# Turning attention weights two units at a time in a merged stage of a hybrid attention layer

## The chip, the cores and the metric

The kernel runs on one core of one Trainium2 chip. The metric is the device time of one execution in microseconds (us); less is better. The core has TensorE (PE: matmuls and transposes), VectorE (DVE), ScalarE (ACT), GpSimd (POOL) and SyncE (SP, which issues most DMAs).

## The reference

One layer for 1024 tokens of width 1024. From the normed input come the operands of two kinds of heads; their outputs are normed, gated, multiplied by `w_out`, normed again and added to the input. The change touches the differential attention of the first kind, 8 heads of width 128:

```python
s = jnp.einsum('bqhmd,bkhmd->bhmqk', qb, k).astype(jnp.float32)   # two maps m per head
p = jax.nn.softmax(jnp.where(mask, s, -jnp.inf), axis=-1)          # causal
w = p[:, :, 0] - lam * p[:, :, 1]
out = jnp.einsum('bhqk,bkhv->bqhv', w.astype(v.dtype), v)
...
oa = rms_norm(oa, subln_g) * (1.0 - lam_init)
oa = oa.reshape(B, S, DA_WIDTH) * jax.nn.silu(ga)
```

The second kind (4 heads of gated linear attention) and the input projection are finished before the stage that the change is in.

## The kernel before

**The stages.** Up to about 645 us the kernel norms the input, multiplies it by `w_in` and runs the linear-attention heads. Then comes a merged stage with all the softmax attention and a part of the product with `w_out`, and at the end the rest of that product, the last norm and the output. To keep float32 accuracy at the speed of the rounded type, each operand of a matmul is split in a high and a low part (`hi`, `lo`), and a product is three matmuls: hi·hi, hi·lo, lo·hi.

**The merged stage.** Three Python generators write its instructions, and `merge` (line 1048) interleaves them: each has a clock of its own, every `yield` of a number moves that clock on by this cost, and the stream with the earliest clock writes next. A `yield` of a function halts its stream until the function holds. Matmuls and transposes are kept in the order in which they are written; the order on ACT, DVE and POOL is fixed when the program is built, and each engine runs its instructions in that order.

- `all_scores` (line 1165): for each head, query blocks of 128 rows from 7 down to 0. `scores` multiplies q by k and ks (the two parts of k) into a bank `sc`, of which three go round; DVE masks and reduces it (L1137) into a row tile `p0` or `p1`; ACT takes the exponential (L1147); POOL (L1153) and DVE (L1152, L1156) combine both maps into the weights, which stay in `p0`. A row over 512 wide has two score pairs. Query blocks 0 to 5 have one `p0` tile each, so the next head's scores of block 5 and of block 3 wait in the stream until the weights of the head before are turned (L1168).
- `all_values` (line 1253): the weights lie with queries on the partitions and must lie with keys there. A **unit** is one key block (or the last two) of one half of a head's queries: ten per head, seven for the upper half (query blocks 4 to 7), three for the lower. `turn` (line 1185) transposes a unit in 3 or 4 transposes into one of two banks `wtr` (`tr_bank` takes them in turns), ACT casts it to `wt_hi` (L1195) and DVE subtracts to `wt_lo` (L1196), three buffers each. `weigh` (line 1199) multiplies it by v into the bank `po`, in three matmuls per key block.
- When a half is complete, ACT copies `po` to `o` (L1290), and `attn_norm` (line 1213) norms it in steps, one per call of `norm_step`: the first squares it on ACT (L1225, L1226), adds on DVE (L1227) and splits the sum into `sq_hl` on ACT (L1228) and DVE (L1229); the fifth sums over the partitions with the matmul `ms`, which takes the next of the two `wtr` banks, and does the rest. In what follows the *upper* and *lower norm* are those of a head's upper and lower half.
- `out_early` (line 1357): parts of the product with `w_out` into the banks `ypart`, a triple of 512-wide matmuls at a time. It fills PE between the other two.

Before the change `all_values` turns one unit at each unit, two ahead of the one that it weighs. Each turn and each weighing is followed by one norm step.

Of the kernel before, what the change touches and what calls it, by code (L numbers as in the profile page):

```python
# [20 lines left out]
DA_HEADS = 8  # L21
# [10 lines left out]
def hymba_kernel(  # L32
# [23 lines left out]
    def fp(t):  # L56
        return t.bitcast(F32)
# [46 lines left out]
    def bank(i, shape, name):  # L104
        return psum.tile(shape, F32, tag=f"b{i}", name=name)
# [13 lines left out]
    def tr(dst, src):  # L119
        tc.keep_in_program_order(pe.transpose(dst, src, ident))  # L120
# [114 lines left out]
    i = order.index((1, 4))  # L235
# [847 lines left out]
    def load_v(h):  # L1083
        v = [smp.tile([P, NT, P], F32R, tag="v", name=f"v{t}", bufs=4) for t in range(2)]
        for t in range(2):

            with tc.issue_after(qk_load[0]) if h else nullcontext():
                ins = sp.dma_start(fp(v[t]), v_d[h // 4][h % 4, t])
            if h == 0:
                tc.keep_in_program_order(ins)  # L1090
        return v
# [9 lines left out]
    def tr_bank(name, shape):  # L1101
        n_tr[0] += 1
        return bank(TR[n_tr[0] % 2], shape, name)
# [77 lines left out]
    def blocks_of(kt, half):  # L1181

        return range(max(kt - 4 * half, 0), 4)

    def turn(h, half, kts):

        pt = tr_bank("wtr", [P, 512])
        n = 0
        for kt in kts:
            for i in blocks_of(kt, half):  # L1190
                tr(pt[:, n : n + P], w[h, 4 * half + i][:, kt * P : (kt + 1) * P])
                n += P
        hi = smp.tile([P, 512], F32R, tag="wt_hi", name="wt_hi", bufs=3)
        lo = smp.tile([P, 512], F32R, tag="wt_lo", name="wt_lo", bufs=3)
        act.copy(hi[:, :n], pt[:, :n])  # L1195
        dve.tensor_tensor(lo[:, :n], pt[:, :n], fp(hi[:, :n]), ALU.subtract)  # L1196
        return hi, lo

    def weigh(po, half, kts, v, wt):

        hi, lo = wt
        n = 0
        for kt in kts:
            ns = len(blocks_of(kt, half)) * P
            for i, (a, b) in enumerate(((v[0], hi), (v[1], hi), (v[0], lo))):
                mm(
                    po[:, 512 - ns :], a[:, kt, :], b[:, n : n + ns],
                    start=(kt == 0 and i == 0), stop=(kt >= 4 * half and i == 2),
                    skip_group_check=True,
                )  # L1210
            n += ns

    def attn_norm(h, half, o):
        if h < DA_HEADS - 1:
            gate = smp.tile([P, 512], F32, tag="gate", name="gate", bufs=2)
        else:
            gate = kp.tile([P, 512], F32, tag=("q1", "k1")[half], name="gate")
        with tc.issue_after(qk_load[0]):
            sp.dma_start(gate, g_d[h][:, cols(half)])
        sq = smp.tile([P, 512], F32, tag="r", name="sq", bufs=1)  # L1220


        hl = smp.tile([P, 512], F32R, tag="sq_hl", name="sq_hl", bufs=1)
        fold = smp.tile([P, 512], F32, tag="fold", name="fold", bufs=1)
        act.activation(fold[:64], o[64:], AF.Square)  # L1225
        act.activation(sq[:64], o[:64], AF.Square)  # L1226
        dve.tensor_tensor(sq[:64], sq[:64], fold[:64], ALU.add)  # L1227
        act.copy(hl[:64], sq[:64])  # L1228
        dve.tensor_tensor(hl[64:], sq[:64], fp(hl[:64]), ALU.subtract)  # L1229
        if h == DA_HEADS - 1:  # L1230

            dve.scalar_tensor_tensor(gate, o, sub_g, gate, ALU.mult, ALU.mult)
        for _ in range(4):
            yield 0.0
        n_tr[0] += 1
        ms = bank(TR[n_tr[0] % 2], [P, 512], "ms")
        mm(ms, ones, hl, start=True, stop=True)
        if h == DA_HEADS - 1 and not half:
            opened[TR[n_tr[0] % 2]] = None
        r = smp.tile([P, 512], F32, tag="r", name="r", bufs=1)  # L1240
        act.activation(r, ms, AF.Ln, bias=eps_t, scale=1.0 / P)
        act.activation(r, r, AF.Exp, scale=-0.5)
        if h < DA_HEADS - 1:
            dve.scalar_tensor_tensor(r, o, sub_g, r, ALU.mult, ALU.mult)
            pool.tensor_tensor(gate, r, gate, ALU.mult)
            sp.dma_start(mixd[h * P : (h + 1) * P, cols(half)], gate)
            stored.append(h)
        else:
            dve.tensor_tensor(gate, gate, r, ALU.mult)
            last_mix[half] = gate  # L1250
        yield 0.0

    def all_values():


        AHEAD = 2
        units = [
            (h, half, kts) for h in range(DA_HEADS) for half in (1, 0)
            for kts in [(k,) for k in range(4 * half + 2)] + [(4 * half + 2, 4 * half + 3)]
        ]  # L1260
        vs, os, turned, norms_todo = {0: v_first}, {}, {}, []
        ahead = iter(units)

        def norm_step():
            while norms_todo:
                c = next(norms_todo[0], None)
                if c is not None:
                    return
                norms_todo.pop(0)

        for i, (h, half, kts) in enumerate(units):
            last = kts[-1] == 4 * half + 3

            ahead_by = AHEAD if h < DA_HEADS - 1 else AHEAD
            while len(turned) < min(i + 1 + ahead_by, len(units)):
                u = next(ahead)
                if u[2] == (0,):
                    yield lambda: (u[0], 4 * u[1]) in w
                turned[u] = turn(*u)
                if u[2][-1] == 4 * u[1] + 3:  # L1280
                    used.add(u[:2])
                yield 0.4
                norm_step()
            if kts == (0,):
                o = smp.tile([P, 512], F32, tag="o", name="o", bufs=3)
                po = bank(PO, [P, 512], "po")
            weigh(po, half, kts, vs[h], turned[h, half, kts])
            norm_step()
            if last:
                act.copy(o, po)  # L1290
                if half and h + 1 < DA_HEADS:
                    vs[h + 1] = load_v(h + 1)
                norms_todo.append(attn_norm(h, half, o))
            yield 0.6

            if i == 1:
                yield SOON * DA_HEADS * 10.0 / T
        carry = norms_todo[-1]
        while len(norms_todo) > 1:
            norm_step()  # L1300
        next(carry)
        yield 0.0
        yield lambda: (ENDS[2], 0) in ps_d
        early_ends()
        yield from carry
# [144 lines left out]
    def early_ends():  # L1450

        for e in range(4, 7):
            last_times(ENDS[2], 0, parts_d[ENDS[2]], e)
        for st in ENDS[:2]:
            last_part(st, parts_d[st])
            for dh in range(2):
                last_times(st, dh, parts_d[st], 7)
        seed(ENDS[2], 1, PO, sums_of(2)[:, 1])
        for st in ENDS[2:4]:
            last_part(st, parts_d[st])  # L1460
# [19 lines left out]
    def last_times(st, dh, part, e):  # L1480
# [14 lines left out]
    merge(  # L1495
        [0.0, T, DA_HEADS * s_cost, all_scores()],
        [LAG - SOON, T + LAG, DA_HEADS * 10.0 * (1 + SOON / T), all_values()],
        [-6.0, T + LAG + 20, 16.0 + 14 * 5.52 + 16 * 2.76 + 11.8, out_early()],
    )
# [124 lines left out]
```

## Time and profile before

| | us |
|---|---|
| three runs, median (lowest to highest) | 974.5 (973.81 to 975.0) |
| the profiled execution | 972.62 |
| its span, first to last instruction | 970.9 |
| PE busy in the span | 951.4 |
| transposes `wtr`, first and last start | 646.4 and 916.4 |

A row of the timeline has the start in us from the span's beginning, the duration in us, the engine, the line of the kernel, the operation, the tile written and the tiles read, the shape and how many were merged into the row; in brackets stands how long the engine had been idle and what released it. A row of a group has busy time and the mean in ns of one; a row of one tile's view has the shortest, the median and the longest duration in ns. Matmuls overlap, so their cost is read from start to start. A matmul's line is 117 and a transpose's 120, whoever called them: they are told apart by their tiles.

### The profile page before, as it was taken

To read this page: it belongs to the slowest core of one execution; us is meant where nothing else is said; L and a number is where in the kernel's file an instruction comes from. 1 tells how busy PE (TensorE), PEld (TensorE's weight loads), DVE (VectorE), ACT (ScalarE), POOL (GpSimd) and SP (SyncE) were. 2 spreads that over 40 slices of the span, in tenths; PEclk is the share of its full clock that TensorE was granted. 3 is DMA by queue.
4 is the path that set the end of the run, shared out by engine and by line. 5 is a ranking of instruction groups with operands and counts; after the bars stand their busy time and mean duration, and the time that the engine had idled before them with its cause. 6 is when DMAs were issued, how large, how long until landed. Compare 5 with 4: busy or idle time off the path is not lost.

```text
span 970.9 us, 15022 instructions
## 1 busy us (share of the span) xinstructions
PE 951.4 (98%) x4946; PEld 810.2 (83%) x4946; DVE 734.9 (76%) x1462; ACT 602.9 (62%) x1164; POOL 205.0 (21%) x263
## 2 busy tenths in 40 slices
PE   6999999999999999999999999999999999999997
PEld 5998988888888888888888888878888888888785
DVE  6986599897687686686766576587888888898554
ACT  8642464764667565576765344366786777887773
POOL 5300001212141221231100002121322222443322
PEclk9999999999999999999999999999999999999999
DMA  9442456478668987996854589988656669995777
GB/s 357 142 124 89 130 171 225 174 247 275 216 202 262 286 277 252 293 293 208 259 184 144 169 249 287 385 273 267 220 172 227 231 201 352 335 293 102 153 210 146
DMA packets 152301, 220.39 MB, mean 227 GB/s; under 512 B 16752, under 2 KB 87408, under 8 KB 152128
## 3 DMA queue, kind: packets, MB, share of 16 engines
q1 hardware_dynamic: 138128, 178.80, 57.2%
q0 software_dynamic: 14096, 40.64, 14.7%
q8 instruction: 39, 0.64, 0.3%
q14 instruction: 38, 0.31, 0.1%
HBM read 133.93 MB, written 88.60 MB: 229 GB/s over the span
## 4 chain that ended last, share of the span: by engine, by line
PE 94%; DVE 3%; ACT 1%; DMA 1%; issue 1%; POOL 0%; SPq 0%; DVEq 0%; ACTq 0%
PE x L117 23%; PE y L117 15%; PE z L117 15%; PE ypart L117 13%; PE sc L117 7%; PE po L117 5%; PE yps L117 4%; PE wtr L120 3%; PE gpo L117 3%; PE kv L117 1%; PE gkl_ps L117 1%; PE pa L117 1%; DMA k_d<-qk_st 1%; PE xT L120 1%; ACT junk L574 0%
## 5 line engine op out<-in xcount | busy, mean ns | idle before, releaser
L352 ACT CAST w<-w_raw 128x512 fp32r<-128x512 f32 (+1 forms) x150 | 98.1, 655 | 91.5 <-PE y L117 47.1
L353 DVE TENSOR_TENSOR w<-w_raw,w 128x512 fp32r<-128x512 f32 (+1 forms) x150 | 109.6, 734 | 40.5 <-ACT w L352 40.1
L1147 ACT ACTIVATE p<-p,stt 128x896 f32<-128x896 f32 (+7 forms) x128 | 99.3, 777 | 36.3 <-DVE stt L1137 33.4
L510 ACT COPY s<-x 128x512 f32<-128x512 f32 x72 | 42.2, 586 | 74.0 <-PE x L117 73.6
L1153 POOL TENSOR_SCALAR p<-p,stt,lam 128x1024 f32<-128x1024 f32 (+3 forms) x64 | 56.0, 875 | 146.8 <-DVE stt L1152 145.1
L677 POOL DMA_DIRECT2D wo_d<-wo_hi x32 | 17.6, 550 | 327.5 <-ACT wo_hi L667 327.5
L1137 DVE CUSTOM_DVE_ANT_0 p<-sc,maskt 128x512 f32<-128x512 f32 (+3 forms) x128 | 74.4, 585 | 14.9 <-PE sc L117 13.7
L117 PE MATMUL z<-s_hi,w 128*128 128x512 f32 x320 | 80.2, 393 | 0.0
L117 PE MATMUL x<-s_hi,w 128*128 128x512 f32 x320 | 80.0, 392 | 0.0
L117 PE MATMUL y<-h_hi,w 128*128 128x512 f32 x320 | 79.9, 392 | 0.0
L117 PE MATMUL ypart<-wo_hi,m_hi 128*128 128x512 f32 x192 | 79.5, 414 | 0.1
L117 PE MATMUL ypart<-wo_hi,m_lo 128*128 128x512 f32 x192 | 75.5, 393 | 0.0
L117 PE MATMUL ypart<-wo_lo,m_hi 128*128 128x512 f32 x192 | 75.4, 393 | 0.0
L333 DVE TENSOR_TENSOR w_raw<-w_raw 128x512 f32<-128x512 f32 (+1 forms) x88 | 65.9, 749 | 10.8 <-DMA w_raw<-in_w_in_dram 9.7
L117 PE MATMUL sc<-k,q 128*128 128x512 f32 (+1 forms) x192 | 69.0, 363 | 1.2 <-DVE stt L1137 1.2
L117 PEld LDWEIGHTS z<-s_hi,w 128*128 128x128 f32 x320 | 59.7, 188 | 12.2
L117 PEld LDWEIGHTS y<-h_hi,w 128*128 128x128 f32 x320 | 59.7, 188 | 12.2
L117 PEld LDWEIGHTS x<-s_hi,w 128*128 128x128 f32 x320 | 59.7, 188 | 12.2
L117 PE MATMUL sc<-ks,q 128*128 128x512 f32 (+1 forms) x192 | 66.1, 347 | 0.0
L1195 ACT CAST wt_hi<-wtr 128x512 fp32r<-128x512 f32 (+1 forms) x80 | 42.8, 535 | 25.3 <-PE wtr L120 24.5
L1196 DVE TENSOR_TENSOR wt_lo<-wtr,wt_hi 128x512 fp32r<-128x512 f32 (+1 forms) x80 | 50.6, 633 | 9.0 <-ACT wt_hi L1195 8.3
L1156 DVE SCALAR_TENSOR_TENSOR p<-p,stt,p 128x1024 f32<-128x1024 f32 (+3 forms) x64 | 52.1, 814 | 4.0 <-POOL p L1153 3.8
(236 smaller groups left out, 2323.7 us busy)
## 6 DMA issues: line engine op xcount, KB each, us to landing
w_raw<-in_w_in_dram SPq DMA_DIRECT2D x48, 512.0 KB, 4.6
wo_d<-wo_hi POOLq DMA_DIRECT2D x32, 256.0 KB, 3.1
q<-q_d SPq DMA_DIRECT2D x32, 256.0 KB, 4.6
k<-k_d SPq DMA_DIRECT2D x32, 256.0 KB, 5.7
ks<-k_d SPq DMA_DIRECT2D x64, 128.0 KB, 6.0
v<-v_d SPq DMA_DIRECT2D x16, 512.0 KB, 7.3
wo_raw<-in_w_out_dram POOLq DMA_DIRECT2D x31, 256.0 KB, 4.6
wo_d<-gqd POOLq DMA_DIRECT2D x22, 256.0 KB, 4.3
```

The lines of the kernel that those rows point to most:

```text
L117: tc.keep_in_program_order(pe.matmul(*a, **k))
L120: tc.keep_in_program_order(pe.transpose(dst, src, ident))
L333: dve.tensor_tensor(dst, a, b, ALU.subtract)
L352: act.copy(w[0], src)
L353: dve.tensor_tensor(w[1], src, fp(w[0]), ALU.subtract)
L510: act.copy(b[k], ps)
L1137: ins = dve.tensor_tensor_reduce(p[:, a:e], sc[:, : e - a], maskt[:, NZ + P - (e - a) :] if last else maskt[:, : e - a], 1.0, 3e38 if i == ...
L1147: act.activation(p[:, :n], p[:, :n], AF.Exp, bias=st[:, m : m + 1], scale=-1.0, accum_out=st[:, 2 + m : 3 + m],)
L1153: pool.tensor_scalar(p1[:, :n], p1[:, :n], st[:, 5:6], lam, ALU.mult, ALU.mult)
L1156: dve.scalar_tensor_tensor(p0[:, :n], p0[:, :n], st[:, 4:5], p1[:, :n], ALU.mult, ALU.subtract)
L1195: act.copy(hi[:, :n], pt[:, :n])
L1196: dve.tensor_tensor(lo[:, :n], pt[:, :n], fp(hi[:, :n]), ALU.subtract)
```

## The change

`turn_two` takes the next two units, waits for the weights of both where a unit is the first of its half, and writes their transposes directly behind one another. It is called once ahead of the loop and then at every second unit, behind its weighing. Before, three units were turned ahead of the first weighing, now two, and then two more behind it. The norm keeps two steps per unit: one directly behind the weighing, and one behind the pair of turns or, at the other units, behind the copy of `o`.

```diff
+        def turn_two():
+            us = [u for _, u in zip(range(2), ahead)]
+            for u in us:
                 if u[2] == (0,):
                     yield lambda: (u[0], 4 * u[1]) in w
+            for u in us:
                 turned[u] = turn(*u)
                 if u[2][-1] == 4 * u[1] + 3:
                     used.add(u[:2])
-                yield 0.4
-                norm_step()
+            yield 0.8
+
+        yield from turn_two()
+        for i, (h, half, kts) in enumerate(units):
+            last = kts[-1] == 4 * half + 3
             if kts == (0,):
...
             weigh(po, half, kts, vs[h], turned[h, half, kts])
             norm_step()
...
-            yield 0.6
+            if i % 2 == 0:
+                yield 0.3
+                yield from turn_two()
+                norm_step()
+                yield 0.3
+            else:
+                norm_step()
+                yield 0.6
```

The same instructions run on every engine, in another order. Three places follow. In these rows a number behind a tile's name only tells tiles of one name apart; it differs between the two kernels.

**First place: the lower norm of head 2.** On PE, the twelve rows that end with its matmul `ms`, before:

```order
L117 MATMUL ypart<-wo_hi,m_hi 128x512
L117 MATMUL ypart<-wo_hi,m_lo 128x512
L117 MATMUL ypart<-wo_lo,m_hi 128x512
L120 MATMUL wtr<-ident,p_7488 128x128
L120 MATMUL wtr<-ident,p_7443 128x128
L120 MATMUL wtr<-ident,p_7361 128x128
L120 MATMUL wtr<-ident,p_7277 128x128
L117 MATMUL sc<-k_7545,q_7542 128x384
L117 MATMUL sc<-ks_7548,q_7542 128x384
L117 MATMUL sc<-k_7553,q_7542 128x512
L117 MATMUL sc<-ks_7556,q_7542 128x512
L117 MATMUL ms<-sq_hl,ones 128x512
```

The same after the change (the pair `sc` at its head ends query block 7 of head 4):

```order
L117 MATMUL sc<-k_7553,q_7550 128x512
L117 MATMUL sc<-ks_7556,q_7550 128x512
L117 MATMUL ypart<-wo_hi,m_hi 128x512
L117 MATMUL ypart<-wo_hi,m_lo 128x512
L117 MATMUL ypart<-wo_lo,m_hi 128x512
L117 MATMUL po<-wt_hi,v_7516 128x512
L117 MATMUL po<-wt_hi,v_7517 128x512
L117 MATMUL po<-wt_lo,v_7516 128x512
L117 MATMUL ms<-sq_hl,ones 128x512
```

`ms` stood behind query block 6's scores and two single turns; it now stands behind the end of query block 7 and one weighing. On DVE, the rows that end with L1229, which `ms` reads, before (`p1` read with `sc` and `stt` is the end of query block 7):

```order
L1137 ISA p1_7719,stt_7717<-sc_7767,maskt_68,stt_7717 128x512
L1137 ISA stt_7717 128x1
L1227 TENSOR_TENSOR sq_7747<-sq_7747,fold_7749 64x512
L1196 TENSOR_TENSOR wt_lo_7781<-wtr_7775,wt_hi_7780 128x512
L1152 RECIPROCAL stt_7717<-stt_7717 128x2
L1229 TENSOR_TENSOR sq_hl_7748<-sq_7747,sq_hl_7748 64x512
```

and after:

```order
L1227 TENSOR_TENSOR sq_7705<-sq_7705,fold_7707 64x512
L1137 ISA p1_7729,stt_7727<-sc_7765,maskt_68 128x512
L1137 ISA stt_7727 128x1
L1137 ISA p1_7729,stt_7727<-sc_7776,maskt_68,stt_7727 128x512
L1137 ISA stt_7727 128x1
L1196 TENSOR_TENSOR wt_lo_7753<-wtr_7747,wt_hi_7752 128x512
L1196 TENSOR_TENSOR wt_lo_7762<-wtr_7756,wt_hi_7761 128x512
L1229 TENSOR_TENSOR sq_hl_7706<-sq_7705,sq_hl_7706 64x512
```

L1229 stood behind one L1196 after that score; it now stands behind both of the pair.

**Second place: query block 5 of head 4**, on PE, where the scores come behind the turn of head 3's last upper unit. Before:

```order
L120 MATMUL wtr<-ident,p_7361 128x128
L120 MATMUL wtr<-ident,p_7277 128x128 x2
L117 MATMUL sc<-k_7553,q_7542 128x512
L117 MATMUL sc<-ks_7556,q_7542 128x512
L117 MATMUL sc<-k_7545,q_7542 128x256
L117 MATMUL sc<-ks_7548,q_7542 128x256
L117 MATMUL sc<-k_7553,q_7542 128x512
L117 MATMUL sc<-ks_7556,q_7542 128x512
L117 MATMUL ypart<-wo_hi,m_hi 128x512
L117 MATMUL ypart<-wo_hi,m_lo 128x512
L117 MATMUL ypart<-wo_lo,m_hi 128x512
```

After:

```order
L120 MATMUL wtr<-ident,p_7659 128x128
L120 MATMUL wtr<-ident,p_7616 128x128
L120 MATMUL wtr<-ident,p_7570 128x128
L117 MATMUL sc<-k_7561,q_7550 128x512
L117 MATMUL sc<-ks_7564,q_7550 128x512
L117 MATMUL sc<-k_7553,q_7550 128x256
L117 MATMUL sc<-ks_7556,q_7550 128x256
L117 MATMUL sc<-k_7561,q_7550 128x512
L117 MATMUL sc<-ks_7564,q_7550 128x512
L117 MATMUL sc<-k_7553,q_7550 128x256
L117 MATMUL sc<-ks_7556,q_7550 128x256
```

The transposes now end a run of seven (units 6 and 7), and the fourth score pair has moved up to directly behind the third; before, a triple `ypart` and a weighing stood between.

**Third place: the upper norm of head 0**, on PE, the rows that end with `ms`. Before:

```order
L117 MATMUL sc<-k_6309,q_6435 128x256
L117 MATMUL sc<-ks_6312,q_6435 128x256
L120 MATMUL wtr<-ident,p_6614 128x128
L120 MATMUL wtr<-ident,p_6569 128x128
L120 MATMUL wtr<-ident,p_6495 128x128
L120 MATMUL wtr<-ident,p_6439 128x128
L117 MATMUL ypart<-wo_hi,m_hi 128x512
L117 MATMUL ypart<-wo_hi,m_lo 128x512
L117 MATMUL ypart<-wo_lo,m_hi 128x512
L117 MATMUL sc<-k_6309,q_6435 128x128
L117 MATMUL sc<-ks_6312,q_6435 128x128
L117 MATMUL ms<-sq_hl,ones 128x512
```

After:

```order
L120 MATMUL wtr<-ident,p_6614 128x128
L120 MATMUL wtr<-ident,p_6584 128x128
L120 MATMUL wtr<-ident,p_6495 128x128
L120 MATMUL wtr<-ident,p_6453 128x128
L117 MATMUL sc<-k_6309,q_6449 128x256
L117 MATMUL sc<-ks_6312,q_6449 128x256
L117 MATMUL ypart<-wo_hi,m_hi 128x512
L117 MATMUL ypart<-wo_hi,m_lo 128x512
L117 MATMUL ypart<-wo_lo,m_hi 128x512
L117 MATMUL sc<-k_6309,q_6449 128x256
L117 MATMUL sc<-ks_6312,q_6449 128x256
L117 MATMUL ms<-sq_hl,ones 128x512
```

The four transposes shown are now the second half of a run of eight. As `ms` takes the older of the two banks, it took that of the unit turned before the last one; now that is the first unit of the same run.

More of the change, by code (lines that the diff above doesn't have):

```diff
@@ L1253, in all_values @@
     def all_values():
-        AHEAD = 2
         units = [
@@ L1269, in norm_step @@
                 norms_todo.pop(0)
[L1271 to L1276, printed above, removed]
+        def turn_two():
+            us = [u for _, u in zip(range(2), ahead)]
+            for u in us:
                 if u[2] == (0,):
                     yield lambda: (u[0], 4 * u[1]) in w
+            for u in us:
                 turned[u] = turn(*u)
```

## The prediction

> **What bounds the kernel now.** I read the page first, then the table of stretches, TensorE's waits, and the timeline where the change lands.
>
> ```profile
> PE 951.4 (98%) x4946; PEld 810.2 (83%) x4946; DVE 734.9 (76%) x1462; ACT 602.9 (62%) x1164; POOL 205.0 (21%) x263
> PE 94%; DVE 3%; ACT 1%; DMA 1%; issue 1%; POOL 0%; SPq 0%; DVEq 0%; ACTq 0%
> ```
>
> TensorE (PE) is busy for 98% of the span and makes up 94% of the chain that ended last. The change lies in the merged stage only, whose transposes run from 646.4 to 916.4 us:
>
> ```profile
> L120 PE MATMUL wtr<-ident,p x288: 270/272/299, 646.4 to 916.4; 128*128 128x128 f32 x144
> L1195 ACT CAST wt_hi<-wtr x80: 455/564/592, 647.2 to 919.3; 128x512 fp32r<-128x512 f32 x48, 128x384 fp32r<-128x384 f32 x32
> L1196 DVE TENSOR_TENSOR wt_lo<-wtr,wt_hi x80: 539/682/693, 648.3 to 919.8; 128x512 fp32r<-128x512 f32 x48, 128x384 fp32r<-128x384 f32 x32
> ```
>
> ```profile
> 700.00:750.00 50.00, 50.00 (x270) 42.67 (x269) 41.48 (x114) 36.18 (x79) 12.25 (x14) 1.00 0.61 195
> 800.00:850.00 50.00, 50.00 (x268) 42.47 (x267) 43.66 (x118) 38.13 (x81) 16.50 (x17) 1.00 1.01 342
> ```
>
> The columns are PE, weight loads, DVE, ACT, POOL, clock. PE has no gap in these stretches, but DVE is busy 41.5 and 43.7 of 50 us, so it has little room to run late. Of PE's waits only two lie in this stage, 1.7 us together:
>
> ```profile
> PE sc L117 <- DVE stt L1137: 1.2, 2, 0.9
> PE po L117 <- ACT wt_hi L1195: 0.5, 1, 0.5
> ```
>
> So a gain must come out of PE's own rows, since hardly a wait is left to remove, and a loss can come from any place where ACT or DVE is no longer in time.
>
> **What grouping saves on PE.** The runs of transposes go from 80 to 40 with the same 288 instructions.
>
> ```profile
> 653.25 0.39 PE L117 MATMUL sc<-ks,q 128*128 128x512 f32 x1
> 653.48 0.60 PE L120 MATMUL wtr<-ident,p 128*128 128x128 f32 x4
> 653.84 0.48 PE L117 MATMUL ypart<-wo_hi,m_hi 128*128 128x512 f32 x1
> 654.15 0.39 PE L117 MATMUL ypart<-wo_hi,m_lo 128*128 128x512 f32 x1
> 654.38 0.39 PE L117 MATMUL ypart<-wo_lo,m_hi 128*128 128x512 f32 x1
> ...
> 18.34 1.91 PE L120 MATMUL xT<-ident,x 128*128 128x128 f32 x16
> ```
>
> A 512-wide matmul takes 0.23 us from start to start (654.15 to 654.38); the first behind a run takes 0.31. Read alone, that is a 0.08 us price for leaving a run, 3.2 us for 40 runs. But the run itself starts the next matmul early. From the run's start to the second matmul behind it is 0.67 us; less that matmul's usual 0.23, four transposes cost 0.44, or 0.11 each. In the one long run, 16 took 1.91: less the last one's 0.27 that is 1.64 over 15 steps, also 0.11. A transpose costs the same in either run. Ends: 0 and 3.2 us; I take **0.1**, by the long run.
>
> **What the moved work does: the lower norm.** Row sums of squares are split on DVE (L1229) and then summed by the matmul ms. Here is the lower half of head 2 before, PE first, then DVE:
>
> ```profile
> 759.91 0.39 PE L117 MATMUL sc<-ks,q 128*128 128x512 f32 x1
> 760.14 0.60 PE L120 MATMUL wtr<-ident,p 128*128 128x128 f32 x4
> ...
> 765.05 0.39 PE L117 MATMUL ms<-sq_hl,ones 128*128 128x512 f32 x1
> ```
>
> ```profile
> 758.48 0.69 DVE L1196 TENSOR_TENSOR wt_lo<-wtr,wt_hi 128x512 fp32r<-128x512 f32 x1
> 759.08 0.68 DVE L1137 CUSTOM_DVE_ANT_0 p<-sc,maskt 128x512 f32<-128x512 f32 x1
> ...
> 760.34 0.75 DVE L1137 CUSTOM_DVE_ANT_0 p<-sc,maskt,stt 128x512 f32<-128x512 f32 x1 [0.31 <-PE sc L117]
> 761.02 0.08 DVE L1137 DVE_READ_ACCUMULATOR2_ANT stt<- 128x1 f32 x1
> 761.02 0.68 DVE L1227 TENSOR_TENSOR sq<-sq,fold 64x512 f32<-64x512 f32 x1
> 761.62 0.68 DVE L1196 TENSOR_TENSOR wt_lo<-wtr,wt_hi 128x512 fp32r<-128x512 f32 x1
> 762.53 0.17 DVE L1152 RECIPROCAL stt<-stt 128x2 f32<-128x2 f32 x1 [0.24 <-ACT p L1147]
> 763.04 1.57 DVE L1229 TENSOR_TENSOR sq_hl<-sq,sq_hl 64x512 fp32r<-64x512 f32 x1 [0.34 <-ACT sq_hl L1228]
> ```
>
> The score that ends query block 7 starts at 759.91, ms 5.14 us later. L1229 ends at 764.61, 0.44 us before ms: no wait, and not much left over. After the change (first place of the order above) PE has between the same two only the rest of that score (0.23), one ypart triple and one po triple (0.69 each): 1.61 us. DVE has L1137, two L1196 and L1229. Rows follow each other some 0.08 before the former's end (758.48 + 0.69 against 759.08), and a releaser costs some 0.04 (759.91 + 0.39 to 760.34). So ms can start 0.39 + 0.04 + 0.68 + 0.60 + 0.60 + 0.69 + 0.04 = 3.04 us behind that score's start: PE waits 3.04 - 1.61 = **1.4 us**. Behind it stand all of PE's later rows; ACT and DVE catch up meanwhile, which gives PE nothing back.
>
> I laid the changed rows of PE, ACT and DVE end to end in the same way at the other lower norms. With one L1196 in place of two the wait is 0.8; where a second ypart triple stands on PE it is 0.7 lower; where L1227 stands behind the score, L1228 on ACT comes between as well. By heads: 0.8, 2.1, 1.4, 0.3, 0.8, 1.4, 0.8, and 0.3 for the upper norm of head 7. Sum **7.9 us**. Ends: 0 (DVE gains room while PE waits, and has 6 us idle in 50) and 15 (an L1229 of 1.57 as above, 0.9 longer, at eight places adds 7).
>
> **The gate of query block 5.** Query block 5 of the next head overwrites a row tile that unit 6 reads, so its scores stand behind that unit's transposes, and now unit 7 is turned with it. Four score pairs, 512, 256, 512, 256 wide, come directly behind a run of seven (second place), on three banks: the fourth pair needs the first one's reduction. From unit 6's last transpose PE has 0.11 + 0.44 (four more) + 0.46 + 0.24 + 0.46 = 1.71 us (256-wide step 0.12):
>
> ```profile
> 716.40 0.28 PE L117 MATMUL sc<-k,q 128*128 128x256 f32 x1
> 716.52 0.28 PE L117 MATMUL sc<-ks,q 128*128 128x256 f32 x1
> ```
>
> ```profile
> L1195 ACT CAST wt_hi<-wtr 128x384 fp32r<-128x384 f32 x32 | 15.1, 473 | 5.4 <-PE wtr L120 4.8 <-PE sc L117 0.3
> L1196 DVE TENSOR_TENSOR wt_lo<-wtr,wt_hi 128x384 fp32r<-128x384 f32 x32 | 17.7, 552 | 2.4 <-ACT wt_hi L1195 2.1
> L1137 DVE CUSTOM_DVE_ANT_0 p<-sc,maskt 128x512 f32<-128x512 f32 x70 | 48.0, 686 | 12.6 <-PE sc L117 12.1
> L1156 DVE SCALAR_TENSOR_TENSOR p<-p,stt,p 128x896 f32<-128x896 f32 x7 | 8.0, 1146 | 0.0
> ```
>
> ACT and DVE need 0.27 + 0.47 + 0.47 + 0.69 + 0.12 for releasers = 2.0: a wait of 0.3. By heads 1 to 7: 0.3, 0.3, 0, 0.3, 1.3, 0.65, 0.65; the longest has the 896-wide L1156 (1.15 us) and a second L1196 among its reductions. Sum **3.5 us**. Ends 0 and 9 (the worst at all seven).
>
> **The upper norm's bank.** ms takes the bank in which the run's first unit was turned (third place). PE has 0.11 + 0.44 + 0.24 + 0.69 + 0.24 = 1.7 us; transpose, cast and L1196 need 0.27 + 0.56 + 0.69 + 0.12 = 1.6. What else ACT or DVE has ahead becomes wait: 1.0 in head 0, 0.7 in head 4, nothing elsewhere. Sum **1.7 us**; ends 0 and 7.
>
> **Sum:** 7.9 + 3.5 + 1.7 - 0.1 = 13.0 us. The profiled execution took 972.62 us (span 970.9), so 985.6; the median of the runs is 974.5, 1.9 above, so **987.5 us**.
>
> [...] In the first 18 us the trace has transposes alone, with waits of about half a microsecond between them:
>
> ```profile
> 6.99 1.09 PE L120 MATMUL xT<-ident,x 128*128 128x128 f32 x4 [6.99 <-DVE x L565]
> ...
> 13.41 4.14 PE L117 MATMUL x<-w,h_hi 128*128 128x256 f32 x16 [0.54 <-ACT h_hi L604]
> ```
>
> There four transposes took 1.09 us, not 0.60, and sixteen 256-wide matmuls 4.14 us, 0.25 each, not 0.12, although the clock column reads 1.00. So transposes did not bring PE to full speed, and 4 us of matmuls at half speed cost about 2 us. [...]
>
> **The rivals.**
> - *Faster.* If the 0.31 us row is a price per run, 3.2 us goes, and if DVE finishes L1229 and the reductions before PE arrives, nothing comes back: 974.5 - 3.2 = 971.3. For it: the slack of 0.44 us and more before. Against it: ms comes 3.5 us earlier relative to the score, more than that slack. It decides from waits under 1.2 us in all. Chance 0.03.
> - *No change.* The waits stay near the saving, 0 to 3 us in all: 974.5. Needs every lower norm to find DVE 1 us ahead of the row count. 0.04. Between this and the forecast, with only the smaller waits: 977 to 980, 0.06.
> - *The clock.* Run and wait together drop PE to half speed at each of the 16 places with a wait (eight, six and two), 2 us each: 987.5 + 32 = 1019.5. Against it: 1.2 us or more of matmuls stand between run and wait, and the waits are 2.1 us at most, while this stage ran at 1.00 with its 80 runs. 0.04.
> - *The change does not do what it says.* The order of PE shows 40 runs of 6 to 8 where it had 80 of 3 or 4, so no chance is given.
>
> The forecast, slower by 6 to 22 us, has 0.83.
>
> **How the numbers follow.** Range 980 to 996: the three sums' middle (half to one and a half of 13 us, 981 to 994) with a little for the 1.57 us rows above; it leaves out some 0.2. About 0.2% is what a measurement here tells from no change: faster 0.03, within 0.2% 0.04, slower 0.93 (0.83 + 0.06 + 0.04).
>
> **What would show it.** In the changed profile PE's waits should gain ms <- DVE sq_hl L1229 (about 8 us, 8 times), sc <- DVE L1137 (3 to 5 us) and ms <- DVE wt_lo L1196 (1 to 2 us), and busy PE time should hold within 2 us of 951. The 512-wide matmul behind a run should still take 0.31 us, 40 times. I am wrong if PE shows no waits for ms, if PE's waits sum to under 5 us, or if the clock or the 0.23 us step changes.

## The result, and the profile after the change

The changed kernel takes **994.4 us** (994.07 to 996.12, 5 runs), the kernel before 974.3 (972.88 to 975.0) on the same chip: 1.0217 times as long [1.0205, 1.0228], 20.1 us more. The forecast was 987.5 (980 to 996). The profiled execution took 994.42 us with a span of 992.7. First the page, engine by engine, and the shares of the chain that ended last:

```profile
PE 957.2 (96%) x4946; PEld 811.9 (82%) x4946; DVE 735.8 (74%) x1462; ACT 603.4 (61%) x1164; POOL 204.9 (21%) x263
PE 81%; DVE 10%; ACT 3%; issue 3%; POOL 2%; DMA 1%; SPq 0%; DVEq 0%; POOLq 0%; ACTq 0%
```

The instructions are as many as before, and DVE is busy as long (735.8 us, before 734.9), but DVE's share of the chain went from 3% to 10%. PE's waits name the rows (what waited, for what: us in total, times, longest):

```profile
PE ms L117 <- DVE sq_hl L1229: 10.3, 8, 3.2
...
PE sc L117 <- DVE stt L1137: 4.5, 9, 1.5
PE ms L117 <- DVE wt_lo L1196: 1.3, 1, 1.3
...
PE ms L117 <- DVE stt L1152: 1.0, 1, 1.0
```

These are the three places of the forecast. Two of the nine waits in the second row lie ahead of the transposes (the longer one, 0.94 us, at 642.16) and stood there before the change too. The last row is the upper norm of head 4, where ms starts 0.14 us behind an L1196, which the profile puts down to the short row behind that. Here is the lower norm of head 2, the place that the prediction worked out, PE and then DVE:

```profile
770.36 0.39 PE L117 MATMUL sc<-ks,q 128*128 128x512 f32 x1
...
771.73 0.39 PE L117 MATMUL po<-wt_lo,v 128*128 128x512 f32 x1
773.60 0.47 PE L117 MATMUL ms<-sq_hl,ones 128*128 128x512 f32 x1 [1.49 <-DVE sq_hl L1229]
```

```profile
770.78 0.75 DVE L1137 CUSTOM_DVE_ANT_0 p<-sc,maskt,stt 128x512 f32<-128x512 f32 x1 [0.46 <-PE sc L117]
...
771.46 1.28 DVE L1196 TENSOR_TENSOR wt_lo<-wtr,wt_hi 128x512 fp32r<-128x512 f32 x2
772.77 0.68 DVE L1229 TENSOR_TENSOR sq_hl<-sq,sq_hl 64x512 fp32r<-64x512 f32 x1
```

PE is through its own rows at 771.96 (771.73 + 0.23), DVE ends the pair of L1196 and L1229 at 773.45, ms starts at 773.60. From start to start PE loses 1.64 us; the row shows 1.49, since the matmul before a wait is shown 0.39 us long and its step is 0.23.

**Where the 20 us are.** From the first transpose to the last, 647.5 to 937.9 us, the stage takes 290.4 us, before 270.0: 20.3 more between unrounded times. Measured from start to start, the 16 places with a wait in it cost 18.3 us: lower norms 11.2, the gate 4.5, the upper norm's bank 2.6. Here are the longest at the gate (head 5, one score pair behind the four) and the longest at the bank (head 0):

```profile
825.38 0.50 PE L117 MATMUL sc<-k,q 128*128 128x512 f32 x1 [1.48 <-DVE stt L1137]
685.37 0.47 PE L117 MATMUL ms<-sq_hl,ones 128*128 128x512 f32 x1 [1.32 <-DVE wt_lo L1196]
```

Before the change no wait of PE as long as 0.1 us lies between the first and the last transpose. The first matmul behind a wait takes 0.31 us, not 0.23 (735.04 to 735.35 at the lower norm of head 1): some 1.3 for 16. And PE ran at half speed once. That is 21.3 with the 1.7 us below; the missing -1.0 is spread thinly over other rows, and I did not trace it. (The profiled executions differ by 21.8 us: this stage also began 1.1 us later, and 0.4 of waiting lie behind its last transpose.) Where no wait is near, the new run costs what the two old ones did:

```profile
727.17 1.03 PE L120 MATMUL wtr<-ident,p 128*128 128x128 f32 x8
727.96 0.48 PE L117 MATMUL ypart<-wo_hi,m_hi 128*128 128x512 f32 x1
728.27 0.40 PE L117 MATMUL ypart<-wo_hi,m_lo 128*128 128x512 f32 x1
```

1.10 us to the second matmul, less its usual 0.23, is 0.87 for eight transposes: 0.11 each, as before.

**One wait was a case of its own.** All engines at the lower norm of head 1, with the scores of head 3's query block 7 in flight:

```profile
733.16 1.20 POOL L1153 TENSOR_SCALAR p<-p,stt,lam 128x1024 f32<-128x1024 f32 x1 [4.05 <-DMA v<-v_d]
733.33 1.56 DVE L1229 TENSOR_TENSOR sq_hl<-sq,sq_hl 64x512 fp32r<-64x512 f32 x1 [0.34 <-ACT sq_hl L1228]
...
735.04 0.47 PE L117 MATMUL ms<-sq_hl,ones 128*128 128x512 f32 x1 [3.20 <-DVE sq_hl L1229]
```

L1229 took 1.56 us instead of 0.69 beside a POOL row, and PE waited 3.2. Then comes this (the columns are as in the prediction's table of stretches; the clock is the 1.00 or 0.50):

```profile
732.20:735.61 3.41, 0.57 (x3) 0.51 (x4) 2.41 (x3) 1.16 (x4) 1.20 (x1) 1.00 1.02 400
735.61:739.02 3.41, 3.41 (x10) 2.64 (x9) 1.97 (x4) 1.26 (x2) 0.08 (x1) 0.50 0.70 254
```

After a stretch in which PE idled for 2.84 us, the clock was 0.50 for 3.41 us: 1.7 us lost.

### The profile page after: what moved, and what is told of

Its sections match the earlier page's. It is cut to its first block, busy times and chain, and to the rows that moved or that the text cites. A ratio compares the mean times of both kernels' runs of the same rounds, so it can differ in the third digit from the quotient of the medians.

```text
span 992.7 us, 15031 instructions
## 1 busy us (share of the span) xinstructions
PE 957.2 (96%) x4946; PEld 811.9 (82%) x4946; DVE 735.8 (74%) x1462; ACT 603.4 (61%) x1164; POOL 204.9 (21%) x263
## 4 chain that ended last, share of the span: by engine, by line
PE 81%; DVE 10%; ACT 3%; issue 3%; POOL 2%; DMA 1%; SPq 0%; DVEq 0%; POOLq 0%; ACTq 0%
PE x L117 22%; PE z L117 15%; PE y L117 14%; PE ypart L117 8%; PE sc L117 5%; PE yps L117 4%; PE po L117 3%; DVE p L1137 3%; PE gpo L117 3%; PE wtr L120 2%; DVE wt_lo L1196 1%; DVE p L1156 1%; POOL p L1153 1%; PE kv L117 1%; ACT p L1147 1%
## 5 line engine op out<-in xcount | busy, mean ns | idle before, releaser
L1153 POOL TENSOR_SCALAR p<-p,stt,lam 128x1024 f32<-128x1024 f32 (+3 forms) x64 | 53.6, 839 | 176.2 <-DVE stt L1152 172.0
L1137 DVE CUSTOM_DVE_ANT_0 p<-sc,maskt 128x512 f32<-128x512 f32 (+3 forms) x128 | 74.0, 583 | 14.1 <-PE sc L117 13.0
L1156 DVE SCALAR_TENSOR_TENSOR p<-p,stt,p 128x1024 f32<-128x1024 f32 (+3 forms) x64 | 52.5, 821 | 14.9 <-POOL p L1153 14.5
L1195 ACT CAST wt_hi<-wtr 128x512 fp32r<-128x512 f32 (+1 forms) x80 | 40.8, 538 | 24.1 <-PE wtr L120 23.9
L1196 DVE TENSOR_TENSOR wt_lo<-wtr,wt_hi 128x512 fp32r<-128x512 f32 (+1 forms) x80 | 49.7, 630 | 6.0 <-ACT wt_hi L1195 5.7
```

What stands on the lines that cost most here:

```text
L1137: ins = dve.tensor_tensor_reduce(p[:, a:e], sc[:, : e - a], maskt[:, NZ + P - (e - a) :] if last else maskt[:, : e - a], 1.0, 3e38 if i == ...
L1153: pool.tensor_scalar(p1[:, :n], p1[:, :n], st[:, 5:6], lam, ALU.mult, ALU.mult)
L1156: dve.scalar_tensor_tensor(p0[:, :n], p0[:, :n], st[:, 4:5], p1[:, :n], ALU.mult, ALU.subtract)
```

## The experiments

The theories. **L** (late rows): two turns side by side put two L1196 in a row on DVE; with the norm and the turns in their new places, L1229, the reductions at the gate and the release of the bank are late, and PE pays each of the three places. **D**: DVE is behind as a whole, and a wait taken away at one row comes back at the next. **R**: the long runs cost PE time. **P**: it is the new place of the turns, behind the weighing, and not the pairing. **C**: waits near runs halve the clock each time. **H**: L1229 took 1.56 us in head 1 because a DVE row with two inputs stands still while a POOL row runs. In the diffs, + and - are against the changed kernel.

### Is it the pairing, its place, or the length of the runs?

Single turns in the new place:

```diff
-        def turn_two():
-            us = [u for _, u in zip(range(2), ahead)]
+        def turn_two(n=2):
+            us = [u for _, u in zip(range(n), ahead)]
...
-            yield 0.8
+            yield 0.4 * n
...
-            if i % 2 == 0:
-                yield 0.3
-                yield from turn_two()
-                norm_step()
-                yield 0.3
-            else:
-                norm_step()
-                yield 0.6
+            yield 0.3
+            yield from turn_two(1)
+            norm_step()
+            yield 0.3
```

> Undone: the pairing alone. One unit is turned behind each weighing, at every unit, two ahead as in the kernel after; the turning keeps the new place behind the weighing, and the norm keeps two steps per unit. Theory L: with one L1196 at a time DVE is not late, PE's waits in the stage fall from 17 to 4 to 7 us, and the time to 979 to 983. Rival P (the new place of the turns and of the norm's steps costs, not the pairing): at least two thirds of the loss stays, 988 or more. Rival R (price of a long run): back to 974 to 977.

Measured: **982.0 us** (980.74 to 982.89), 1.0076 of before [1.0062, 1.009]. PE's waits:

```profile
PE ms L117 <- DVE sq_hl L1229: 2.5, 2, 2.0
PE sc L117 <- DVE stt L1137: 1.7, 3, 0.9
...
PE po L117 <- ACT wt_hi L1195: 0.9, 1, 0.9
PE wtr L120 <- DVE wt_lo L1196: 0.9, 1, 0.9
```

The pairing makes 12.4 of the 20.1 us; 7.7 stay with the new place alone. P wanted 988 or more, so it falls as the main cause, and R wanted 974 to 977. The forecast had not parted pairing and place.

Two turns still at every second unit, with room for other work between them:

```diff
                 if u[2][-1] == 4 * u[1] + 3:
                     used.add(u[:2])
-            yield 0.8
+                yield 0.4
```

> Two units are still turned at every second unit, but with a step of 0.4 on the values' clock between them, so that another stream's matmuls may come between the two runs: 3 or 4 transposes per run, as before the change. Theory L: the two L1196 still fall within about 1 us of each other ahead of L1229, so the ms waits stay at 6 to 9 us; the gate's waits fall by 2 to 3 us since scores can pass between the two. 986 to 991. Rival R (the length of a run is what costs): 974 to 977, for no run is longer than before. Rival D: 988 to 994.

Measured: **990.3 us** (989.54 to 991.63), 1.0167 [1.0153, 1.018].

```profile
PE ms L117 <- DVE sq_hl L1229: 8.2, 6, 3.3
PE sc L117 <- DVE stt L1137: 1.8, 3, 0.9
```

But for one run of six, no run of transposes here is longer than before the change, yet 16 of 20 us remain: R is out. What counts is that two turns fall close together ahead of L1229: ms <- L1229 is down by 2.1 us only (10.3 to 8.2), and the gate, where scores now pass between the two, by 2.7 (4.5 to 1.8).

### The wait of ms for L1229, taken away

L1229 still runs, but nobody reads what it writes: the low part of the squares is left out of the norm.

```diff
-        dve.tensor_tensor(hl[64:], sq[:64], fp(hl[:64]), ALU.subtract)
+        dve.tensor_tensor(fold[64:], sq[:64], fp(hl[:64]), ALU.subtract)
...
-        mm(ms, ones, hl, start=True, stop=True)
+        mm(ms, ones[:64], hl[:64], start=True, stop=True)
```

> Undone: the wait of ms on L1229 alone. L1229 keeps its place and its work on DVE, but writes to rows that nobody reads, and ms sums only the 64 rows of the high part (the low part of the squares is left out of the norm). PE's order is the same as after the change, row for row. After 994.4, before 974.3. Theory L (two L1196 side by side make DVE late for three named rows of PE, each of which PE pays separately): the eight waits ms <- L1229 go, 10.3 us as shown, 11.6 from start to start, and with them the half clock of 3.4 us behind the one of 3.2 us (1.7); what stays is sc <- L1137 and the waits for the bank. So 981 to 984. Rival D (DVE as a whole is behind after the pairing, and ms is only the first row that shows it): DVE's work is unchanged, so the wait moves on to sc <- L1137 and PE still loses 15 us or more: 990 to 994. Rival R (the long runs themselves cost PE time): 990 to 994, with no waits in PE's table.

Measured: **990.2 us** (989.27 to 991.68), 1.0165 [1.0151, 1.0179]: where D put it. PE's waits in the stage fell by some 7.5 us, the time by 4.3. The row of ms in its tile's view, shortest, median and longest ms in ns, shows where part of it went:

```profile
L117 PE MATMUL ms<-sq_hl,ones x16: 462/498/502, 684.7 to 946.9; 64*128 64x512 f32 x16
```

With half the rows, ms is shown 498 ns long, at places without a wait too; in the next kernel, with 128 rows, the median is 398. The kernel also ran a stretch at half clock (a granted clock of 0.97 over 700 to 750 us). So the edit had costs of its own, and I made it again with ms 128 rows high:

```diff
-        hl = smp.tile([P, 512], F32R, tag="sq_hl", name="sq_hl", bufs=1)
+        if not hl_once:
+            hl_once.append(smp.tile([P, 512], F32R, tag="sq_hl", name="sq_hl", bufs=1))
+            pool.memset(fp(hl_once[0][64:]), 0.0)
+        hl = hl_once[0]
...
-        dve.tensor_tensor(hl[64:], sq[:64], fp(hl[:64]), ALU.subtract)
+        dve.tensor_tensor(fold[64:], sq[:64], fp(hl[:64]), ALU.subtract)
```

> The same undoing as in the kernel whose ms summed 64 rows, without that kernel's own cost. L1229 keeps its place on DVE and writes to rows that nobody reads (the low part of the squares is left out of the norm), and ms reads all 128 rows, the lower 64 of which were zeroed once. PE's order is that after the change. In the 64-row kernel PE's waits fell by 7.5 us in the stage, but its ms and their two neighbours took longer from start to start, by 0.3 to 0.4 us at 14 of 16 places, some 5 us. Theory L: without that, 984 to 986: 11.6 us of waits less, 2 us of them come back as waits for L1228 and the gate, and the half clock behind head 1's wait may stay or go (1.7). Rival D (DVE as a whole is behind, so a wait taken away comes back at the next row): 988.5 or more, with the 64-row matmul costing nothing.

Measured: **985.6 us** (985.14 to 986.15), 1.0121 [1.0106, 1.0136].

```profile
PE sc L117 <- DVE stt L1137: 6.1, 9, 1.3
PE ms L117 <- ACT sq_hl L1233: 2.0, 2, 1.5
PE ms L117 <- DVE wt_lo L1196: 1.5, 2, 1.3
```

```profile
L117 PE MATMUL ms<-sq_hl,ones x16: 389/398/501, 685.3 to 943.1; 128*128 128x512 f32 x16
```

(L1233 is L1228 of the changed kernel.) This one removal gives back 8.8 us. Of the 10.3 us of waits 2.0 stayed at two of the same ms, which now wait for ACT's half of the split, so far hidden behind DVE's. Another 0.2 is the bank of a third ms. Only some 1.8 came back at other rows, nearly all of it at the gate (4.5 to 6.1): L holds for most of it, D for about a sixth.

### The gate

Both kernels have this edit; the second one has the first edit of the section above as well (64 rows).

```diff
-            yield 0.8
+                if u[1:] == (1, (6, 7)):
+                    yield 0.4
+            yield 0.4 if us and us[0][1:] == (1, (6, 7)) else 0.8
```

> Only the gate: a step of 0.4 on the values' clock between the turns of units 6 and 7 of an upper half, all else as after the change. Theory L: sc <- L1137 falls from 4.5 us to 2 to 2.5, the ms waits stay at 10 to 11 us, the half clock behind head 1 too: 990.5 to 992.5. Rival D (what is taken away here comes back at ms): 994 to 995, with ms waits of 12 us or more.

> As the kernel without the low part in ms, and in addition a step of 0.4 on the values' clock between the turns of units 6 and 7 of an upper half, so that query block 5's scores can come between the two (the runs of 6 to 8 are cut in two at this one place per head). Theory L: the waits sc <- L1137 behind the gate, 4.5 us in 16.., fall to some 2; the waits for the bank of the upper norm stay at about 2. So 978.5 to 981.5, 2 to 3 below the kernel with the first edit alone. Rival D: no change against that kernel, since DVE has the same work. Rival R: one run in five is split, so a fifth of 20 us, 4 us, against the first kernel, and no more.

Measured: **991.4 us** (989.98 to 993.4), 1.0182 [1.0166, 1.0198], and **986.9 us** (985.76 to 988.99), 1.0132 [1.0118, 1.0146]. The waits of the first:

```profile
PE ms L117 <- DVE sq_hl L1229: 10.4, 8, 3.2
...
PE sc L117 <- DVE stt L1137: 2.8, 5, 1.2
```

The edit is worth 3.1 us alone and 3.3 on top of the other, and ms <- L1229 stays at 10.4, so here D is wrong: what the gate gives is not lost at ms. The second kernel missed its absolute number only because the kernel it stands on had. Added up, 8.8 us for ms and 3.1 for the gate come close to the 12.4 that single turns gave back.

### The norm, later and earlier

The number of steps that the norm waits before its ms is 4. Eight, without and with the gate's edit:

```diff
-        for _ in range(4):
+        for _ in range(8):
             yield 0.0
```

> Only the norm's eight steps in place of four; the gate's runs stay whole. Theory L: ms <- L1229 gone, sc <- L1137 at 5 to 8 us, no half clock: 980 to 984, 3 to 5 above the kernel with both edits. Rival D: 988 or more, the wait moving on to sc.

> All work and the pairs of the change are kept; two numbers are changed. The norm waits eight steps in place of four before its ms, and a step of 0.4 stands between the turns of units 6 and 7 of an upper half. Theory L: ms comes long after L1229 and after the banks are free, and the scores of query block 5 pass between the two turns: no wait for L1229 over 0.5 us, sc <- L1137 at 2 to 4 us, 976 to 980. Rival P (turning behind the weighing costs by itself, as with single turns: 982): 982 or more. Rival R (long runs cost): 988 or more.

Measured: **992.6 us** (991.12 to 996.16), 1.0204 [1.018, 1.0227], and **987.1 us** (986.03 to 988.36), 1.0136 [1.0121, 1.0152]. Both miss by 7 us or more. The waits for L1229 are gone as expected, but in the second kernel, gate edit and all:

```profile
PE sc L117 <- DVE stt L1137: 8.0, 6, 2.5
```

Its timeline of DVE at the gate of query block 5, where PE waits 2.53 us from 703.2 on, for the reduction at 705.12:

```profile
702.55 1.47 DVE L1229 TENSOR_TENSOR sq_hl<-sq,sq_hl 64x512 fp32r<-64x512 f32 x1 [0.34 <-ACT sq_hl L1228]
704.05 1.15 DVE L1156 SCALAR_TENSOR_TENSOR p<-p,stt,p 128x896 f32<-128x896 f32 x1
705.12 0.68 DVE L1137 CUSTOM_DVE_ANT_0 p<-sc,maskt 128x512 f32<-128x512 f32 x1
```

DVE is still at L1229 there (long again: POOL's L1153 ran from 702.39 to 703.48) and then at the 896-wide L1156. In the changed kernel the same norm's L1229 was done long before its gate, where PE waited 0.25 us:

```profile
694.73 0.69 DVE L1229 TENSOR_TENSOR sq_hl<-sq,sq_hl 64x512 fp32r<-64x512 f32 x1
```

```profile
707.45 0.38 PE L117 MATMUL sc<-k,q 128*128 128x256 f32 x1 [0.25 <-DVE stt L1137]
```

So the edit moves more than ms. `norm_step` works on the oldest norm alone, and with eight steps the upper norm is not through when the lower half is complete; the lower norm starts three calls later. On DVE its L1229 stands behind two more L1196 and four more reductions (L1137) than in the changed kernel, in heads 0 to 5 of both kernels, which puts it at the gate. In the kernel with eight steps alone sc <- L1137 sums to 11.6 us. D's number came out, but its mechanism isn't shown by these two runs: PE no longer pauses at ms and so comes to the gate sooner, as D has it, and DVE has rows of the norm there that it did not have before, which is L's order again. The runs do not part the two. Both forecasts had overlooked the move.

Two steps:

```diff
-        for _ in range(4):
+        for _ in range(2):
             yield 0.0
```

> The norm waits two steps in place of four, so its ms comes one unit earlier, of the lower and of the upper norms. Theory L: ms <- L1229 grows to 20 to 28 us at 11 to 14 places and the time to 1005 to 1013; the clock halves only behind a wait of about 3 us or more, 0 to 3 times. Rival C (a wait near a run halves the clock each time, for the 3.4 us seen once after the change, 1.7 us of time): 10 or more halvings, 1020 to 1030. Rival D (DVE is the bound and PE only waits for what DVE has not done yet): no more than 997, as DVE's work is the same.

Measured: **1011.0 us** (1009.08 to 1013.92), 1.0384 [1.0364, 1.0403].

```profile
PE ms L117 <- DVE sq_hl L1229: 20.1, 11, 3.1
...
PE sc L117 <- DVE stt L1137: 6.6, 10, 2.0
```

As L had it: DVE's work is the same, and 16.6 us are lost by an earlier ms. Not all of them are waits: the profiled execution has six stretches of 3.41 us at half clock, four of them in the stage, where the changed kernel has one (the drop at the very end, which the kernels before and after the change have too, is not counted). Its granted clock is 0.989 over 1012.2 us, the changed kernel's 0.996 over 992.7, or some 22 and 8 us at half clock with the end. C falls, as the clock did not halve at each of the 20 or so waits; but L had expected three at most, behind waits of 3 us, and one of the four stands behind 2.01 us of idling (last section).

### The row of 1.56 us

One row of POOL moved to ACT, first in a head beside whose row nothing waits, which makes it the control (both kernels leave the factor `lam` out of that block's weights):

```diff
+                    if (h, qb) == (2, NT - 1):
+                        act.activation(p1[:, :n], p1[:, :n], AF.Copy, scale=st[:, 5:6])
+                    else:
                         pool.tensor_scalar(
                             p1[:, :n], p1[:, :n], st[:, 5:6], lam, ALU.mult, ALU.mult
                         )
```

> One row of the kernel after the change is moved: the scaling of p1 (L1153) in query block 7 of head 2 runs on ACT in place of POOL (and leaves out the factor lam in that one block's weights). PE's and DVE's orders are the same, row for row; on ACT one row more stands behind L1228. In the profile after the change this POOL row (1.20 us) started 0.17 us ahead of head 1's L1229, which took 1.56 us in place of 0.69, and ms waited 3.2 us. Theory H (a DVE row with two inputs stands still while a POOL row runs): L1229 takes 0.69 there, that wait falls to 2.3 us; if the clock halves only where some 2.2 us or more of waiting fall in one of its 3.41 us stretches, it halves in some executions and not in others. 991 to 994. Rival (L1229 was long for another reason, such as its own wait for ACT): 1.5 us and 3.2 us again, 994 to 995.

In the other kernel the 2 in the first line is a 3:

> The run before moved the POOL row of head 2's query block 7, but the row beside head 1's lower norm is that of head 3's query block 7 (the scores run two heads ahead of the norm). Here that one runs on ACT in place of POOL, without the factor lam; PE's and DVE's orders are those after the change. The run before is the control: the same edit, at a row beside which nothing waits, left time, L1229 (1.56 us) and the wait of 3.2 us as they were. Theory H (a DVE row with two inputs stands still while a POOL row runs): L1229 takes 0.69 us, the longest ms wait falls from 3.2 to 2.3 us, and the half clock behind it goes in most executions: 991.5 to 993.5. Rival (L1229 is long for its own wait for ACT's L1228): 1.5 us and 3.2 us, 994 to 995.

Measured: **994.1 us** (993.18 to 995.37), 1.0206 [1.0191, 1.022], nothing changed; and **992.4 us** (991.36 to 994.63), 1.0189 [1.0175, 1.0203]. In the second, all sixteen L1229 (there L1232) are short, and the longest wait is 0.9 us less:

```profile
L1232 DVE TENSOR_TENSOR sq_hl<-sq,sq_hl x16: 684/684/1560, 681.4 to 948.7; 64x512 fp32r<-64x512 f32 x16
```

```profile
L1232 DVE TENSOR_TENSOR sq_hl<-sq,sq_hl x16: 684/685/687, 681.3 to 945.8; 64x512 fp32r<-64x512 f32 x16
```

```profile
PE ms L117 <- DVE sq_hl L1232: 9.7, 8, 2.3
```

The first row is the control's, the other two are of the kernel with head 3's row moved. In this kernel's profile PE's clock stays at 1.00 behind that wait. H holds for this row.

L1229 on POOL:

```diff
-        dve.tensor_tensor(hl[64:], sq[:64], fp(hl[:64]), ALU.subtract)
+        pool.tensor_tensor(hl[64:], sq[:64], fp(hl[:64]), ALU.subtract)
```

> L1229 moves from DVE to POOL, all work kept; PE's order is the same. A POOL row of 512 columns with two inputs takes 1.30 us (L1245), on DVE L1229 took 0.69. Theory L with H: ms no longer waits behind the two L1196, but for a row twice as long, which in head 1 stands behind L1153; and DVE's rows with two inputs stand still for it. ms waits of 5 to 9 us in place of 10.3, the gate unchanged: 988 to 993. Rival D (DVE has too much work): 11 us less on DVE give 982 to 986.

Measured: **992.8 us** (991.4 to 993.44), 1.0193 [1.0178, 1.0207].

```profile
PE ms L117 <- POOL sq_hl L1229: 6.8, 7, 2.5
PE sc L117 <- DVE stt L1137: 5.5, 10, 1.5
PE ms L117 <- DVE wt_lo L1196: 2.9, 2, 2.2
```

16 rows less on DVE (busy 724.3 us in place of 735.8) gain 1.7 us, where D wanted 8 or more. It is not the amount of DVE's work alone that sets the time: on POOL the row takes about twice as long (median 1.28 us, on DVE 0.69), and ms still waits for it.

No version here beats the kernel before; 982.0 us is the nearest. Between the transposes of the stage before, PE had no wait left that a reordering could win.

## Why the prediction was right, and where its sizes were off

- **Grouping saves 0.1 us.** Held: 0.87 us for eight transposes, 0.11 each. The faster rival (971.3) rested on a price per run, which is not there, and on small waits; they sum to 18 us.
- **Lower norm, 7.9 us.** The term that was furthest off, though right in mechanism and place (eight waits, ms <- L1229): 11.2 us in the stage and 0.4 behind its last transpose, 11.6. Two sizes of the step were off. From the end of L1229 to ms took 0.15 us, not 0.04; and L1229 starts 0.03 us behind the end of the L1196 ahead of it, without the 0.08 of overlap that the working took. Together 0.2 at each norm, 1.8 us. Another 0.87 is what a POOL row added to L1229 in head 1 (forecast 2.1, measured 3.36), as the run without that row showed; the last 1.0 is spread over the heads. The prediction quoted such a 1.57 us row and put it only in the bounds (up to 7 us); which place meets it hangs on POOL.
- **The gate, 3.5 us.** Measured 4.5, the heads' shape as forecast (head 5 longest, 2.2 us in its two waits, forecast 1.3). Half of the sum, though, does not lie at the fourth score pair, on which the working rests: in heads 5 and 6 the waits of 1.6 and 0.7 us from start to start stand at the first pair of the next query block. Splitting the run there gave 3.1 us back.
- **The upper norm's bank, 1.7 us.** Measured 2.6 at the two heads named (0 and 4): 1.5 and 1.1.
- **Not in the sum:** the first matmul behind a wait, 0.08 us longer, some 1.3 us; and the half clock, 1.7 us.
- **The clock rival.** Priced at 2 us for each of 16 waits with a chance of 0.04; a stretch at half clock came once, behind the wait that the POOL row made longest, and cost 1.7 us. That waits of 2.1 us at most speak against it was the author's estimate: in the early-norm kernel half clock came behind 2.01 us of idling.
- **What would show it.** The three wait rows came as named, 10.3, 4.5 and 2.3 us, where about 8, 3 to 5 and 1 to 2 were written. PE's busy time missed its mark, 957.2 for 951 within 2: a 512-wide row at half clock is shown 0.63 us long (736.40), not 0.39, and a row before a wait counts with its 0.39, not its step of 0.23.
- **Two sentences that did not hold.** One is that ACT and DVE catching up in a wait gives PE nothing back: with the waits for L1229 gone, 1.8 of 10.3 us came back at other rows. The terms were priced one by one and added, but they are not quite independent. The other is that two of PE's waits before the change lie in this stage: they lie at 640.98 and 919.81, just outside the transposes.
- **Luck.** All three terms of waiting, and what was not in the sum, were off to the same side, by 7 us together; that 994.4 still lies in the range is owed to its upper end, which was set by half as much again of the sum and a little for long L1229 rows, and so only in small part for these causes.

What stays open: why single turns in the new place still cost 7.7 us. Their waits, 6.0 us by the four rows shown, lie at four different kinds of row (before the change 1.7 us at two), the granted clock is 0.97 over 900 to 950 us, and I took none of them away. Open too is how much of the wait at the gate, with the norm later, is the missing pause and how much the moved rows.

## What to carry to other kernels

Before work for a second engine is bunched on a full first one, count the rows of the second that stand between a result and its reader, and not the busy shares: here DVE was at 74 to 76% of the span in both kernels and its order cost most of the 20 us. Before a wait is removed by moving its reader, see what moves along with it, and at which row the next reader in line will find the engine; price the moves together. Look at what runs on POOL beside a DVE row that PE waits for.

## What the runs showed of the hardware

**An L1229 on DVE that started beside an L1153 on POOL ended 0.53 to 0.57 us behind it.** L1229 reads two tiles from SBUF, and alone it takes 0.685 us; started 0.17 us behind a POOL row of 1.20 it took 1.56, and with that row on ACT 0.69. The rest of the POOL row (1.03) and then 0.53 us make up the 1.56. Before the change four L1229 started with 0.33 to 1.04 us of an L1153 left and took 0.87 to 1.57, that rest and 0.54; three with 0.15 or less left took 0.68. L1156, which reads two tiles as well, took 1.06 in place of 0.75 beside an L1153 (at 683.57 in the changed kernel). Beside L1419 of POOL, which only issues a DMA, an L1229 (at 923.78 in the changed kernel) took 0.68, and L1196, which reads a bank and one tile of SBUF, never took more than 0.693 in that kernel, though 14 of its 512-wide rows started while a POOL row ran. It goes the other way too: L1245 on POOL, 1.30 us in the median, took 2.27 at 813.72 in the changed kernel, 0.17 us behind the start of an L1156 of 1.28. And on POOL, L1229 took 1254 to 1998 ns:

```profile
L1229 POOL TENSOR_TENSOR sq_hl<-sq,sq_hl x16: 1254/1282/1998, 680.0 to 945.7; 64x512 fp32r<-64x512 f32 x16
```

**Half clock came in stretches of 3.41 us.** By the clock record of the changed kernel's trace, the drop in the stage lasts 3.413 us and begins 252.59 us, 74 times 3.413, ahead of the drop at the end. So I cut the stage on this grid and looked at how long PE was idle in one stretch, by the rows as shown. Behind a stretch with 2.84 us in the changed kernel the next ran at half clock; behind one with 1.78 (885.80 to 889.21) it did not. There is no sharp limit in these numbers: the first kernel with ms of 64 rows, whose waits in the stage are 1.5 us at most, has its clock of 0.97 over 700 to 750 us. The length of a wait alone doesn't decide. Here 2.01 us of waiting in the early-norm kernel (3.41 less PE's 1.40) fell into one stretch:

```profile
679.38:682.79 3.41, 1.40 (x7) 0.95 (x6) 2.63 (x7) 1.70 (x4) 0.43 (x1) 1.00 0.87 237
682.79:686.21 3.42, 3.42 (x11) 3.04 (x10) 2.39 (x6) 1.65 (x4) 1.61 (x2) 0.50 0.03 12
```

and here a wait of some 2.5 us, in the kernel with the later norm and the gate's edit, straddles two (1.81 and 0.72), and the clock of the next stays at 1.00:

```profile
885.55:888.96 3.41, 1.60 (x10) 1.08 (x8) 2.86 (x5) 1.75 (x5) 1.96 (x2) 1.00 0.52 126
888.96:892.37 3.41, 2.69 (x15) 2.29 (x16) 2.55 (x10) 1.23 (x3) 0.00 (x0) 1.00 0.55 67
```

The executions of one kernel differ in this too: with eight steps the granted clock was 0.996 in those of 991.1 and 991.3 us, 0.993 in that of 993.8 and 0.992 in that of 996.2; with the wait for L1229 taken away (ms 128 rows high) it was 0.998 or 0.999 in all four, 985.1 to 986.2 us.
